# Residual stream by tokens instead of by features in a three-layer transformer kernel on one core

## The chip, the cores and the metric

The kernel runs on one core of a Trainium2 chip. A core has TensorE (PE, matrix products), VectorE (DVE), ScalarE (ACT), GpSimd (POOL) and SyncE (SP, which here issues transfers), each with an instruction stream of its own that it works off in order. The metric is the device time of one execution in microseconds; for the kernel before it is the median of three runs.

## The reference, cut to what matters

512 tokens of 1024 features go through three layers, all in float32. Layer A is attention with a forget gate and a squared-ReLU MLP; layers B and C each have a mixer of two branches and a SwiGLU block. What matters here is what stands at the end of each branch: a product with an output matrix, its addition to the residual stream `x`, and the next normalization over the 1024 features of each token.

```python
# layer A
x = x + g_m * y                                   # y = attention @ fox_w_out
h = rms_norm(x, norm_mlp[i]) * (1 + sc_f) + sh_f
x = x + g_f * (jnp.square(jax.nn.relu(h @ w_mlp_in[i])) @ w_mlp_out[i])
...
# layers B and C
x = x + gate_m * rmsnorm(mixers[layer](h), post_m)
h = rmsnorm(x, pre_f) * (1.0 + scale_f) + shift_f
x = x + gate_f * rmsnorm(swiglu(h, *ffns[layer]), post_f)
```

`rms_norm` divides by the root of the mean square over a token's features. In B and C the branch's output `y` is normalized too, before it is added.

## The kernel before

**Products.** Every float32 matrix is held as two float32r parts, `hi` and `lo`, and a product is three matmuls, hi by hi (L116), hi by lo (L117), lo by hi (L118). A weight unit is loaded by SyncE (`wraw`), rounded by ScalarE (`whi`, L148) and its rest formed by VectorE (`wlo`, L149); names with an x are a second ring. "Feature-major" means features on the partitions and tokens along the row (`fm`, L165), "token-major" the reverse (`tm`, L173).

**The residual stream** `x` and the branch's sum `yacc` are feature-major, 8 chunks of 128 features by 512 tokens. The normalized `h` is kept feature-major as pairs `h_hi`, `h_lo`, since the next products contract over features.

**The six places.** Twice per layer, in its middle (mixer to MLP or SwiGLU) and at its end (to the next layer's mixer, or to the output), `down_halves` (L1283) makes a branch's last product by halves of 256 tokens: per half eight chunks of 24 matmuls with 256 columns. VectorE takes each chunk out of PSUM (L1334, in A L709), ScalarE squares it, GpSimd adds the squares up (L356), the last square stays apart. `total` (L318) then sums over the partitions on TensorE with matrices of ones, three matmuls (L327, L328, L330) and for the last square two passes. `rstd` makes the reciprocal root from a logarithm, an exponential and one Newton step. In B and C `post` (L1265) adds the normalized `yacc` to `x` and sums squares again; `modulate` (L359) forms `u` (L373), `h_hi` (L374, ScalarE) and `h_lo` (L378). While the second half goes through these steps, TensorE has the next block's products with the first half's tokens: `two_blocks` (L1307) computes seven output chunks by halves (`by_halves`) and one in full width.

**What sets the order.** A list scheduler writes each engine's stream by the order in which the program emits instructions and by priority. `behind(n)` lets what is emitted in it give way to the next n instructions; the table `LAG` holds n for the totals, by place and half. Scratch tiles (`t`) come from one ring of `nt` buffers of 512 columns. PSUM has four banks `mm`, in the MLP and SwiGLU phases three `mm2` and one `tot`.

## Time and profile before

| | us |
|---|---|
| median of three runs | 2395.36 |
| lowest and highest | 2389.12, 2403.04 |
| the profiled execution, span from first to last instruction | 2392.9 |
| TensorE busy | 2262.0 |
| VectorE busy | 1508.8 |
| ScalarE busy | 1062.9 |
| GpSimd busy | 439.5 |

TensorE's mean granted clock over the span is 0.970 of full speed. The page gives no separate time of the profiled execution, so its span stands for it; it lies inside the spread of the three runs. A busy share is an average over stages: what matters at the six places is which engine the others wait for there, and whether TensorE, which works in order, stands still.

### The profile page before, as it was taken

To read this page: it belongs to the slowest core of one execution; us is meant where nothing else is said; L and a number is where in the kernel's file an instruction comes from. 1 tells how busy PE (TensorE), PEld (TensorE's weight loads), DVE (VectorE), ACT (ScalarE), POOL (GpSimd) and SP (SyncE) were. 2 spreads that over 40 slices of the span, in tenths; PEclk is the share of its full clock that TensorE was granted. 3 is DMA by queue.
4 is the path that set the end of the run, shared out by engine and by line. 5 is a ranking of instruction groups with operands and counts; after the bars stand their busy time and mean duration, and the time that the engine had idled before them with its cause. 6 is when DMAs were issued, how large, how long until landed. Compare 5 with 4: busy or idle time off the path is not lost.

```text
span 2392.9 us, 35221 instructions
## 1 busy us (share of the span) xinstructions
PE 2262.0 (95%) x13328; PEld 1963.2 (82%) x13328; DVE 1508.8 (63%) x3180; ACT 1062.9 (44%) x2089; POOL 439.5 (18%) x446
## 2 busy tenths in 40 slices
PE   5999998999999898999999999799999998999997
PEld 5898888788898676888888889767888888888887
DVE  6888876664536997675654655735888457422424
ACT  4677654344334554254432233344666344332222
POOL 3333230100013310322000001412343012000002
PEclk7999999999999999999999999899999999999999
DMA  7344326655533223033364652342011242331411
GB/s 249 113 145 138 98 84 199 223 195 166 176 108 88 69 65 56 1 118 94 115 220 150 200 178 80 87 121 79 30 45 33 92 137 71 106 106 60 134 55 61
DMA packets 246090, 271.88 MB, mean 114 GB/s; under 512 B 18736, under 2 KB 204752, under 8 KB 245920
## 3 DMA queue, kind: packets, MB, share of 16 engines
q1 hardware_dynamic: 238192, 254.03, 33.6%
q0 software_dynamic: 3424, 11.26, 2.0%
q10 hardware_dynamic: 4304, 4.34, 0.6%
q8 instruction: 105, 1.72, 0.3%
q14 instruction: 65, 0.53, 0.1%
HBM read 261.16 MB, written 8.42 MB: 113 GB/s over the span
## 4 chain that ended last, share of the span: by engine, by line
PE 75%; DVE 14%; ACT 4%; DMA 3%; issue 2%; POOL 1%; SPq 0%; POOLq 0%; DVEq 0%; ACTq 0%
PE mm L116 21%; PE mm L118 21%; PE mm L117 21%; PE tp L431 2%; DVE wlo L149 1%; DMA wraw<-l_w_in 1%; DVE u L1275 1%; DVE p L421 1%; PE mm L1734 1%; ACT whi L148 1%; PE mm L1657 1%; PE o L470 1%; DVE u L373 1%; PE o L469 1%; PE mm L605 1%
## 5 line engine op out<-in xcount | busy, mean ns | idle before, releaser
L116 PE MATMUL mm<-h_hi,whi 128*128 128x512 f32 (+2 forms) x1056 | 373.8, 356 | 17.9 <-ACT h_hi L374 12.6
L117 PE MATMUL mm<-h_lo,whi 128*128 128x512 f32 (+2 forms) x1056 | 373.3, 354 | 0.2 <-DVE h_lo L378 0.2
L118 PE MATMUL mm<-h_hi,wlo 128*128 128x512 f32 (+2 forms) x1056 | 372.9, 353 | 0.1
L148 ACT CAST whi<-wraw 128x1024 fp32r<-128x1024 f32 (+1 forms) x196 | 199.7, 1023 | 228.4 <-PE mm L117 146.7
L149 DVE TENSOR_TENSOR wlo<-wraw,whi 128x1024 fp32r<-128x1024 f32 (+3 forms) x172 | 210.0, 1224 | 137.2 <-ACT whi L148 136.0
L116 PEld LDWEIGHTS mm<-h_hi,whi 128*128 128x128 f32 (+1 forms) x1056 | 202.5, 193 | 49.9 <-ACT h_hi L374 14.4
L118 PEld LDWEIGHTS mm<-h_hi,wlo 128*128 128x128 f32 (+1 forms) x1056 | 203.8, 193 | 28.1 <-DVE wlo L149 0.5
L116 PE MATMUL mm<-h_hi,whix 128*128 128x512 f32 (+1 forms) x648 | 224.8, 348 | 1.4 <-DVE yacc L1334 1.4
L117 PEld LDWEIGHTS mm<-h_lo,whi 128*128 128x128 f32 (+1 forms) x1056 | 204.0, 193 | 26.6 <-DVE h_lo L378 0.5
L117 PE MATMUL mm<-h_lo,whix 128*128 128x512 f32 (+1 forms) x648 | 224.1, 346 | 0.0
L118 PE MATMUL mm<-h_hi,wlox 128*128 128x512 f32 (+1 forms) x648 | 223.8, 346 | 0.0
L116 PE MATMUL mm<-whi,h_hi 128*128 128x256 f32 x672 | 202.7, 302 | 0.3 <-DVE mod_modA L823 0.3
L117 PE MATMUL mm<-wlo,h_hi 128*128 128x256 f32 x672 | 194.8, 290 | 0.2 <-DVE wlo L149 0.2
L118 PE MATMUL mm<-whi,h_lo 128*128 128x256 f32 x672 | 194.2, 290 | 0.3 <-DVE h_lo L799 0.2
L117 PE MATMUL mm<-hid,whi 128*128 128x512 f32 (+1 forms) x544 | 185.8, 342 | 3.8 <-DVE hid L112 3.8
L116 PE MATMUL mm<-hid,whi 128*128 128x512 f32 (+1 forms) x544 | 187.0, 347 | 1.0 <-ACT hid L109 1.0
L149 DVE TENSOR_TENSOR wlox<-wraw,whix 128x1024 fp32r<-128x1024 f32 x106 | 135.0, 1281 | 81.0 <-ACT whix L148 79.5
L118 PE MATMUL mm<-hid,wlo 128*128 128x512 f32 (+1 forms) x544 | 185.5, 342 | 0.0
L148 ACT CAST whix<-wraw 128x1024 fp32r<-128x1024 f32 x106 | 109.0, 1034 | 143.4 <-PE mm L117 96.9
L246 DVE SCALAR_TENSOR_TENSOR ada_acc<-ada,cols,ada_acc 128x512 f32<-128x512 f32 x182 | 136.3, 749 | 50.9 <-DMA ada<-l_ada_w 43.5
L116 PE MATMUL mm<-hid,whix 128*128 128x256 f32 (+1 forms) x432 | 145.5, 337 | 2.1 <-DVE x L709 2.1
L117 PE MATMUL mm<-hid,whix 128*128 128x256 f32 (+1 forms) x432 | 145.0, 336 | 0.0
(466 smaller groups left out, 5248.9 us busy)
## 6 DMA issues: line engine op xcount, KB each, us to landing
ada<-l_ada_w SPq DMA_DIRECT2D x192, 256.0 KB, 4.5
wraw<-l_w_in SPq DMA_DIRECT2D x54, 512.0 KB, 3.8
wraw<-l_w_gate SPq DMA_DIRECT2D x44, 512.0 KB, 4.2
wraw<-l_w_up SPq DMA_DIRECT2D x44, 512.0 KB, 4.1
wraw<-l_w_down SPq DMA_DIRECT2D x40, 512.0 KB, 3.5
wraw<-w_mlp_in SPq DMA_DIRECT2D x32, 512.0 KB, 4.0
wraw<-w_mlp_out SPq DMA_DIRECT2D x32, 512.0 KB, 3.6
hid<-w_ada SPq DMA_DIRECT2D x48, 256.0 KB, 5.5
```

The costliest lines, as they stand in the source:

```text
L116: mm(ps, a[0], b[0], start=start, stop=False)
L117: mm(ps, a[0], b[1], start=False, stop=False)
L118: mm(ps, a[1], b[0], start=False, stop=stop)
L148: nc.scalar.copy(hi[:, :nk, :n], raw[:, :nk, :n])
L149: e.tensor_sub(lo[:, :nk, :n], raw[:, :nk, :n], hi[:, :nk, :n].bitcast(F32))
L246: nc.vector.scalar_tensor_tensor(acc, raw, c, acc, op0=OP.mult, op1=OP.add)
L373: nc.vector.scalar_tensor_tensor(u, x[:, k, t], gs[:, k:k + 1], r, op0=OP.mult, op1=OP.mult)
L421: nc.vector.tensor_scalar(p[:, :n], p[:, :n], st[:, 2:3], None, op0=OP.mult)
L431: nc.tensor.transpose(tp[:w, j * 128:(j + 1) * 128], p[:, j * 128:j * 128 + w], self.ident)
L469: nc.tensor.matmul(o[:, oc], a, pt[:, j, 0, c], start=first and j == 0, stop=False)
L470: nc.tensor.matmul(o[0:64, oc], a[:, 0:64], pt[:, j, 1, c], start=False, stop=False)
L605: nc.tensor.matmul(S[:, :n], qs[hi, e, tb], kl[hi, :n], start=False, stop=False)
```

## The change

`x` and `yacc` become token-major: 4 blocks of 128 tokens, each a row of 1024 features per token. `down_blocks` replaces `down_halves`: by pairs of token blocks, for each half of the features and each block a token-major product of 24 matmuls with 512 columns. A block's evictions add to `yacc` or `x`; ScalarE squares 512 features and accumulates them per token into a column of `stats`; `token_rsqrt` makes the reciprocal root of that column on VectorE in eleven operations. Gate and gain vectors, which were columns, are needed as rows on all partitions: `row` writes them to DRAM, `on_all` loads them broadcast, both on GpSimd's queue. `normalized` scales a block of `x` by its column on ScalarE into two tiles `xn`, and `modulate` transposes the tiles of a pair of blocks on TensorE into `tot`, from where ScalarE (`h_hi`) and VectorE (`u`, `h_lo`) make the feature-major pairs.

The other products that add to `yacc` (`down`, `out_early`) turn token-major too, with 512 columns as before. Weight units of more than 256 columns hold 2 rows of 128 by 512 columns instead of 4 by 256. `two_blocks` makes six chunks by halves and two in full width; the PSUM banks are two `mm2` and two `tot`. The ring of scratch tiles is 8 in layer A's MLP (12 before) and 8 in the SwiGLU phases (7 before). The host lays out `x` in both ways and reads the output token-major.

```diff
-LAG = ((50, 150), (100, 150), (120, 160), (60, 290), (60, 100), (60, 190))
+LAG = ((110, 130), (110, 130), (110, 130), (110, 130))
+AT, NT = 8, 8
...
+        step = 2 if sum(c1 - c0 for c0, c1 in cols) > 256 else 4
+        for i, k0 in enumerate(range(ks[0], ks[1], step)):
+            out += self.unit(w, k0, min(step, ks[1] - k0), cols, aux[i] if isinstance(aux, tuple) else aux, gain)
...
+    def squares(self, st, i, v):
+        junk = self.t("sq")
+        self.nc.scalar.activation(junk, v, AF.Square, accum_out=st[:, i:i + 1])
+    def token_rsqrt(self, st):
+        nc = self.nc
+        v, h, r, t = [st[:, i:i + 1] for i in (2, 3, 4, 5)]
+        nc.vector.tensor_add(v, st[:, 0:1], st[:, 1:2])
+        nc.vector.tensor_scalar(h, v, -0.5 / D, -0.5 * EPS, op0=OP.mult, op1=OP.add)
+        ri = r.bitcast(I32)
+        nc.vector.tensor_scalar(v, h, -2.0, None, op0=OP.mult)
+        nc.vector.tensor_scalar(ri, v.bitcast(I32), 1, None, op0=OP.arith_shift_right)
+        nc.vector.tensor_scalar(ri, ri, -1.0, float(0x5F3759DF), op0=OP.mult, op1=OP.add)
+        for _ in range(3):
+            nc.vector.tensor_scalar(t, r, r, h, op0=OP.mult, op1=OP.mult)
+            nc.vector.scalar_tensor_tensor(r, t, 1.5, r, op0=OP.add, op1=OP.mult)
+        return r
+    def stats(self):
+        return self.tmp.tile([128, 6], F32, name="stats", bufs=6)
+    def modulate(self, xns, gs, sh, pair, lag=0):
+        nc = self.nc
+        t = slice(pair * 256, pair * 256 + 256)
         us = []
         for k in range(KD + MLAG):
             if k < KD:
+                if k % 2 == 0:
+                    ps = self.tot.tile([128, 2, 256], F32, name="tot")
+                    with self.behind(lag):
+                        for e in range(2):
+                            c = (k + e) % 4 * 128
+                            for b in range(2):
+                                nc.tensor.transpose(ps[:, e, b * 128:b * 128 + 128], xns[b][k // 4][:, c:c + 128], self.ident)
+                p = ps[:, k % 2]
                 u = self.t("u")[:, :256]
                 us.append(u)
+                nc.scalar.activation(self.h[k][0][:, t], p, AF.Identity, scale=gs[:, k:k + 1], bias=sh[:, k:k + 1])
+                nc.vector.tensor_scalar(u, p, gs[:, k:k + 1], sh[:, k:k + 1], op0=OP.mult, op1=OP.add)
             if k >= MLAG:
+                hi, lo = self.h[k - MLAG]
+                nc.vector.tensor_sub(lo[:, t], us[k - MLAG], hi[:, t].bitcast(F32))
+    def normalized(self, x, b, st):
+        r = self.token_rsqrt(st)
+        out = []
+        for c in range(2):
+            out.append(self.t("xn"))
+            self.nc.scalar.activation(out[-1], x[:, b, c * 512:c * 512 + 512], AF.Copy, scale=r)
+        return out
+    def row(self, name, cols):
+        d = self.dram.tile([KD, 128], F32, name=f"row_{name}")
+        self.nc.gpsimd.dma_start(d.rearrange("k p -> p k"), cols)
+        return d
+    def on_all(self, d):
+        t = self.tmp.tile([128, D], F32, name="row", bufs=1)
+        self.nc.gpsimd.dma_start(t, d.rearrange("(o k) p -> o (k p)", o=1).to_broadcast([128, D]))
+        return t
...
+    def gated(self, x, row, early=None):
+        nc = self.nc
+        def evict(b, c, ps, st):
+            f = slice(c * 512, c * 512 + 512)
+            u = self.t("u")
+            if early and c:
+                nc.vector.tensor_add(u, early[b], ps)
+                ps = u
+            nc.vector.tensor_mul(u, ps, row[:, f])
+            nc.vector.tensor_add(x[:, b, f], x[:, b, f], u)
+            self.squares(st, c, x[:, b, f])
         return evict
...
+        ready, late = self.two_blocks([load(0), load(1)], h)
+        y = self.aux.tile([128, 4, D], F32, name="yacc")
...
+                row = self.on_all(self.row("gA5", self.mod("modA", 5)))
+                self.down_blocks(w2, g * 8, hid, self.gated_sum(x, y, row), after)
...
-        self.ph = self.phase("mlpA", (("mm2", 3), ("tot", 1)), nt=12)
-        x = self.reload(a["x"])
+        self.ph = self.phase("mlpA", (("mm2", 2), ("tot", 2)), nt=AT)
+        x, rowA = self.reload(a["xt"]), self.on_all(rowA)
...
+        def mid(b, st):
+            self.xn[b % 2] = self.normalized(x, b, st)
+            if b % 2:
+                self.modulate(self.xn, gs2, self.mod("modA", 3), b // 2, LAG[0][b // 2])
+        self.down_blocks(a["fox_w_out"][0], 0, cat, self.gated(x, rowA, self.early), mid, done=FE)
...
+        def go(b, st):
+            if b == 0:
                 self.mv = self.mod_vectors(l)
-            self.modulate(x, self.mv["gm"], self.mv["sm"], half, ss, lag and lag[half])
-            self.spill(x, d, half)
+            self.xn[b % 2] = self.normalized(x, b, st)
+            self.spill(x, d, b)
+            if b % 2:
+                self.modulate(self.xn, self.mv["gm"], self.mv["sm"], b // 2, lag[b // 2])
...
+    def post(self, x, y, row, b, st, sums=True):
+        nc = self.nc
+        r = self.token_rsqrt(st)
+        st = self.stats() if sums else None
+        for c in range(2):
+            f = slice(c * 512, c * 512 + 512)
+            u = self.t("u")
+            nc.vector.scalar_tensor_tensor(u, y[:, b, f], r, row[:, f], op0=OP.mult, op1=OP.mult)
+            nc.vector.tensor_add(x[:, b, f], x[:, b, f], u)
+            if sums:
+                self.squares(st, c, x[:, b, f])
+        return st
...
+    def down_blocks(self, w, k0, xs, evict, after, gain=None, done=0):
+        first = [0, done]
+        ws = [self.weights(w, (k0 + first[c], k0 + KD), [(c * 512, c * 512 + 512)], c == 1, gain) for c in range(2)]
+        self.xn = [None, None]
+        for pair in range(2):
+            st = [self.stats() for _ in range(2)]
+            for c in range(2):
+                for e in range(2):
+                    b = pair * 2 + e
+                    ps = self.mm.tile([128, T], F32, name="mm")
+                    self.tm(ps, ws[c], 0, 512, xs[first[c]:], b)
+                    evict(b, c, ps, st[e])
+                    if c:
+                        after(b, st[e])
...
+        ps = [[self.mm.tile([128, T], F32, name="mm") for _ in range(4)], [self.mm2.tile([128, T], F32, name="mm2") for _ in range(2)]]
+        part = lambda pp, w, cs: [(p, w[i // 2], i % 2 * 128) for p, i in zip(pp, cs)]
+        self.by_halves([part(ps[0], ws[0], range(4)), part(ps[1], ws[1], (0, 2))], xs)
+        def late(i):
+            p = self.mm.tile([128, T], F32, name="mm")
+            self.fm(p, ws[1][i // 2], i % 2 * 128, i % 2 * 128 + 128, xs)
+            return p
+        return [ps[0], [ps[1][0], None, ps[1][1], None]], late
...
-        self.ph = self.phase(f"ffn{l}", (("mm2", 3), ("tot", 1)), nt=7)
-        x = self.reload(d)
-        def mid(half, ss):
-            ss = self.post(x, y, m["pm"], half, ss, LAG[2][half])
-            self.modulate(x, m["gf"], m["sf"], half, ss, LAG[3][half])
-        self.down_halves(w, 0, cat, self.add_to(y), "ssy", mid, self.col["ssm_g" if l == 0 else "gla_g"])
+        self.ph = self.phase(f"ffn{l}", (("mm2", 2), ("tot", 2)), nt=NT)
+        x, pm = self.reload(d), self.on_all(pm)
...
+        def mid(b, st):
+            st = self.post(x, y, pm, b, st)
+            self.xn[b % 2] = self.normalized(x, b, st)
+            if b % 2:
+                self.modulate(self.xn, m["gf"], m["sf"], b // 2, LAG[2][b // 2])
+        self.down_blocks(w, 0, cat, self.add_to(y), mid, self.col["ssm_g" if l == 0 else "gla_g"])
+        pf = self.on_all(self.row(f"pf{l}", m["pf"]))
         self.next_modulation(l + 1)
         self.ada_lag = ADA
-        go = self.into(x, l + 1, LAG[5])
+        go = self.into(x, l + 1, LAG[3])
         self.ffn(self.h, *[a[f"l{l}_{n}_2"] for n in ("w_gate", "w_up", "w_down")], y,
-                 lambda half, ss: go(half, self.post(x, y, m["pf"], half, ss, LAG[4][half], self.has(l + 1))))
+                 lambda b, st: go(b, self.post(x, y, pf, b, st, self.has(l + 1))))
```

The order of instructions at the second half of B's middle shows the move. TensorE before, among the next block's products with the first half's tokens; `tot_11664` is the total of the second half's squares of `yacc`:

```order
L118 MATMUL mm_11816<-h_hi_61,wlo_11777 128x256
L116 MATMUL mm_11817<-h_hi_61,whi_11776 128x256
L327 MATMUL tot_11664<-ss_hi_11660,onesr_86 128x256 [waits Activation_49]
L117 MATMUL mm_11817<-h_lo_62,whi_11776 128x256
L118 MATMUL mm_11817<-h_hi_61,wlo_11777 128x256
L328 MATMUL tot_11664<-ss_lo_11661,onesr_86 128x256 [waits DVE_49]
L116 MATMUL mm_11818<-h_hi_61,whi_11788 128x256
L330 MATMUL tot_11664<-sq_last_11657,onesr_86 128x256
L117 MATMUL mm_11818<-h_lo_62,whi_11788 128x256
L118 MATMUL mm_11818<-h_hi_61,wlo_11789 128x256
```

TensorE after, at the same point; `xn_11172` and `xn_11237` are the normalized blocks 2 and 3, `mm_11346` and the next are the SwiGLU's first chunks for these tokens:

```order
L119 MATMUL mm2_11351<-h_hi_61,wlox_11343 128x256
L399 MATMUL tot_11241<-ident_82,xn_11237 128x128 [waits Activation_49]
L399 MATMUL tot_11241<-ident_82,xn_11172 128x128
L399 MATMUL tot_11241<-ident_82,xn_11237 128x128
L399 MATMUL tot_11252<-ident_82,xn_11237 128x128
L399 MATMUL tot_11252<-ident_82,xn_11172 128x128
L399 MATMUL tot_11252<-ident_82,xn_11237 128x128
L117 MATMUL mm_11346<-h_hi_61,whi_11300 128x256 [waits Activation_49]
L117 MATMUL mm_11347<-h_hi_61,whi_11300 128x256
```

The total of three matmuls, which stood between products that need nothing of it, is gone. The transposes (two more for block 2 stand seventeen rows ahead) stand behind all products with the first pair's tokens, and the products behind them need their result. What the rows wait for stands in brackets.

VectorE before, at the end of the update of `x` in the second half, with the root of the total `tot_11725`:

```order
L1275 SCALAR_TENSOR_TENSOR u_11711<-yacc_9672,pm0_7391,r_11659 128x256
L1278 TENSOR_TENSOR x_10991<-x_10991,u_11711 128x256
L112 TENSOR_TENSOR ss_lo_11722<-ssx_11674,ss_hi_11721 128x256
L306 SCALAR_TENSOR_TENSOR nr_11731<-r_11720 128x256
L307 SCALAR_TENSOR_TENSOR nr_11731<-tot_11725,nr_11731 128x256
L308 SCALAR_TENSOR_TENSOR r_11720<-nr_11731,r_11720 128x256
L373 SCALAR_TENSOR_TENSOR u_11735<-x_10991,gf0_7389,r_11720 128x256
L373 SCALAR_TENSOR_TENSOR u_11738<-x_10991,gf0_7389,r_11720 128x256
```

VectorE after, for block 3: `stats_11054` is the column of the branch's output, `stats_11215` that of `x` after the update:

```order
L1339 SCALAR_TENSOR_TENSOR u_11216<-yacc_9425,stats_11054,row_10747 128x512
L1340 TENSOR_TENSOR x_10744<-x_10744,u_11216 128x512
L1339 SCALAR_TENSOR_TENSOR u_11221<-yacc_9425,stats_11054,row_10747 128x512
L1340 TENSOR_TENSOR x_10744<-x_10744,u_11221 128x512
L372 TENSOR_TENSOR stats_11215<-stats_11215 128x1
L373 TENSOR_SCALAR stats_11215<-stats_11215 128x1
...
L379 TENSOR_SCALAR stats_11215<-stats_11215 128x1
L380 SCALAR_TENSOR_TENSOR stats_11215<-stats_11215 128x1
L404 TENSOR_SCALAR u_11246<-tot_11241,gf0_7141,mod_mod0_4827 128x256
L407 TENSOR_TENSOR h_lo_62<-u_11246,h_hi_61 128x256
```

Each column `stats` is worked on by eleven rows, of which the excerpt leaves out seven in the second one. In the stream before, three operations of 256 columns stood in its place.

## Rows read from the trace of the kernel before

**Rows 1.** The page, busy time of each engine in the whole span.

```profile
span 2392.9 us, 35221 instructions
...
PE 2262.0 (95%) x13328; PEld 1963.2 (82%) x13328; DVE 1508.8 (63%) x3180; ACT 1062.9 (44%) x2089; POOL 439.5 (18%) x446
```

**Rows 2.** The page, shares of the chain that ended last.

```profile
PE 75%; DVE 14%; ACT 4%; DMA 3%; issue 2%; POOL 1%; SPq 0%; POOLq 0%; DVEq 0%; ACTq 0%
```

**Rows 3.** TensorE's waits over the whole span: us in total, times, longest.

```profile
PE tot L327 <- ACT ss_hi L109: 21.7, 8, 4.5
PE mm L116 <- ACT h_hi L374: 12.6, 4, 3.5
...
PE mm L116 <- DVE x L709: 3.0, 2, 2.1
...
PE mm L116 <- DVE yacc L1334: 1.8, 2, 1.4
```

**Rows 4.** Timeline of TensorE, 512 columns: start us, modelled us; 35 rows between.

```profile
1439.64 0.39 PE L117 MATMUL mm<-h_lo,whi 128*128 128x512 f32 x1
...
1447.80 0.39 PE L117 MATMUL mm<-h_lo,whi 128*128 128x512 f32 x1
```

**Rows 5.** Timeline of TensorE, 256 columns, 42 rows between.

```profile
1475.76 0.28 PE L117 MATMUL mm<-hid,whix 128*128 128x256 f32 x1
...
1480.92 0.28 PE L118 MATMUL mm<-hid,wlox 128*128 128x256 f32 x1
```

**Rows 6.** Timeline of TensorE, a total over partitions and the product after it.

```profile
1482.65 0.28 PE L327 MATMUL tot<-ss_hi,onesr 128*128 128x256 f32 x1
...
1483.13 0.47 PE L116 MATMUL mm<-hid,whi 128*128 128x256 f32 x1
```

**Rows 7.** Timeline of TensorE, two groups of four 128x128 transposes.

```profile
984.39 0.60 PE L1235 MATMUL mm<-ident,y 128*128 128x128 f32 x4
984.83 0.60 PE L1166 MATMUL mm<-ident,hid 128*128 128x128 f32 x4
```

**Rows 8.** Timeline of mixer B: squares on ScalarE, column chain on VectorE.

```profile
1038.84 0.63 ACT L1226 ACTIVATE z<-y 128x512 f32<-128x512 f32 x1 [1.96 <-DVE y L1224]
...
1039.38 0.18 ACT L1226 ACTIVATION_READ_ACCUMULATOR z<-y 128x1 f32 x1
...
1039.60 0.15 DVE L1227 TENSOR_SCALAR st<-st 128x1 f32<-128x1 f32 x1 [0.19 <-ACT z L1226]
...
1041.48 0.58 DVE L882 SCALAR_TENSOR_TENSOR st<-rs_t,rs_y 128x1 f32<-128x1 f32 x1
```

**Rows 9.** Costliest groups of VectorE by shape: xcount | busy us, mean ns.

```profile
L149 DVE TENSOR_TENSOR wlo<-wraw,whi 128x1024 fp32r<-128x1024 f32 x164 | 206.1, 1260 | 134.6 <-ACT whi L148 133.4
...
L1334 DVE TENSOR_TENSOR yacc<-yacc,mm 128x256 f32<-128x256 f32 x64 | 26.3, 415 | 51.4 <-PE mm L118 51.4
...
L709 DVE SCALAR_TENSOR_TENSOR x<-mm,mod_modA,x 128x512 f32<-128x512 f32 x24 | 17.9, 748 | 15.6 <-PE mm L118 15.5
...
L1368 DVE TENSOR_TENSOR yacc<-yacc,mm 128x512 f32<-128x512 f32 x16 | 10.9, 682 | 10.8 <-PE mm L118 10.8
```

**Rows 10.** Timeline of TensorE, a wait at B's middle.

```profile
1132.90 0.58 PE L327 MATMUL tot<-ss_hi,onesr 128*128 128x256 f32 x1 [3.56 <-ACT ss_hi L109]
```

**Rows 11.** Busy time by stretch: length, PE (x) ..., PEclk, DMA.

```profile
1132.00:1136.00 4.00, 3.10 (x12) 2.92 (x13) 0.42 (x1) 1.08 (x3) 0.41 (x1) 0.50 0.43 127
1456.00:1568.00 112.00, 98.31 (x726) 93.25 (x725) 72.08 (x140) 43.17 (x88) 36.46 (x49) 0.94 0.32 91
1940.00:2060.00 120.00, 109.67 (x814) 105.38 (x813) 79.32 (x159) 58.20 (x119) 22.83 (x26) 0.97 0.36 110
```

**Rows 12.** Timeline of the tail: last product, last addition.

```profile
2378.68 0.28 PE L118 MATMUL mm<-hid,wlox 128*128 128x256 f32 x1
...
2389.16 0.42 DVE L1278 TENSOR_TENSOR x<-x,u 128x256 f32<-128x256 f32 x1
```

**Rows 13.** DMA issues: queue, xcount, KB each, median us to landing.

```profile
x<-sp_l POOLq DMA_DIRECT2D x4, 1024.0 KB, 8.0
```

More of the change, by code (lines that the diff above doesn't have):

```diff
@@ L143, in unit @@
             return out
-        hi, lo = self.ring(aux)
+        hi, lo = (wide(t) for t in self.ring(aux))
         if gain is None:
@@ L279 @@
     mv = None
+    row_p = None
     ada_tile = None
@@ L516, in fox_early @@
         self.finish()
[L517 to L525 removed]
+        wk = self.weights(w, (0, FE), [(512, 1024)])
+        for b in range(4):
+            ps = self.mm.tile([128, T], F32, name="mm")
+            self.tm(ps, wk, 0, 512, cat[:FE], b)
+            out.append(self.hid.tile([128, T], F32, name="hid"))
+            self.nc.scalar.copy(out[-1], ps)
+            yield
     def fox_gates(self, h):
@@ L1283, in down_halves @@
-    def down_halves(self, w, k0, xs, evict, name, after, gain=None, done=0):
-        first = [0, 0, done, done]
-        ws = [self.weights(w, (k0 + first[q], k0 + KD), [(q * 256, q * 256 + 256)], q >= 2, gain) for q in range(4)]
-        for half in range(2):
-            t0, t1 = half * 256, half * 256 + 256
-            ss = self.sums(name)
-            for m in range(KD):
-                ps = self.mm.tile([128, T], F32, name="mm")
-                self.fm(ps, ws[m // 2], m % 2 * 128, m % 2 * 128 + 128, xs[first[m // 2]:], t0, t1)
-                v = evict(m, ps[:, t0:t1], slice(t0, t1))
-                sums = self.add_squares(ss, v, m)
-            after(half, sums)
+        r = self.token_rsqrt(st)
@@ new lines, in post, with down @@
+        st = self.stats() if sums else None
+        for c in range(2):
+            f = slice(c * 512, c * 512 + 512)
+            u = self.t("u")
+            nc.vector.scalar_tensor_tensor(u, y[:, b, f], r, row[:, f], op0=OP.mult, op1=OP.mult)
+            nc.vector.tensor_add(x[:, b, f], x[:, b, f], u)
+            if sums:
+                self.squares(st, c, x[:, b, f])
+        return st
+    def down(self, w, k0, xs, y, first, step):
+        for c in range(2):
+            wk = self.weights(w, (k0, k0 + len(xs)), [(c * 512, c * 512 + 512)], aux=c == 1)
+            for b in range(4):
+                ps = self.mm.tile([128, T], F32, name="mm")
+                self.tm(ps, wk, 0, 512, xs, b)
+                v = y[:, b, c * 512:c * 512 + 512]
+                if first:
+                    self.nc.scalar.copy(v, ps)
+                else:
+                    self.nc.vector.tensor_add(v, v, ps)
+                self.step(step)
@@ L1348, in ffn @@
                     self.step()
-                    gate, up = [ready[p][i] if p < 2 else self.chunk(ws, i, h) for i in (c, 2 + c)]
+                    gate, up = [(ready[p][i] or late(i)) if p < 2 else self.chunk(ws, i, h) for i in (c, 2 + c)]
                     s = self.t("f", F32)
```

163 lines of the change are left out of this document (45 added, 118 removed).

## Prediction

> **What bounds the kernel now.** I read the page's busy times first. TensorE is busy for 2262.0 of 2392.9 us, VectorE for 63%, GpSimd for 18% [rows 1]; the reader is to see that work taken from GpSimd or ScalarE can't show in the time unless something waits for it. The chain of waits says the same from the other side: three quarters of it is TensorE, 14% is VectorE [rows 2]. So a change pays in two coins only: the time that TensorE needs to issue its matmuls, and the time that it stands still. The list of TensorE's waits gives the second. The largest are those of the totals L327 for `ss_hi` (21.7 us in 8) and of the next products for the first `h_hi` of a half (12.6 us in 4), with 3.0 for `x` and 1.8 for `yacc` from evictions: 39.1 us, all at the six places where a residual branch ends and the next block begins [rows 3]. The table by stretches places them: at B's end TensorE is idle for 13.7 of 112 us, at C's middle for 10.3 of 120 [rows 11]. These are the places that the change rewrites.
>
> **TensorE's own time.** The order counts 2352 matmuls of 256 columns fewer in the products at the six places (2208 in the last products, 144 in the blocks by halves that become full-width) and 1176 of 512 more. A matmul's modelled duration is longer than its slot, so I take start to start: 36 steps of 512 columns take 8.16 us, 0.2267 each [rows 4]; 43 steps of 256 take 5.16, 0.120 each [rows 5]. 2352 x 0.120 = 282.2 becomes 1176 x 0.2267 = 266.6: -15.6 us. The 18 totals go, each 0.48 from its first matmul to the product behind it [rows 6]: -8.6. The 160 transposes come, 0.44 for four [rows 7]: +17.6. Sum -6.6.
>
> Against the largest of these terms, the Trainium skill (TensorE: Matmul & The Clock Gate, Back-to-back issue gap) gives an isolated gap of N/2.4 + 2.5 ns; an estimate from it is 216 ns at 512 columns and 109 at 256. By that, two narrow matmuls would cost only 3 ns more than a wide one, the term would be 1176 x 0.003 = -3.5 instead of -15.6, and the sum would end 12 us later. The rows differ from it in both widths and decide, since they are these products on this chip.
>
> **VectorE at the six places.** Per token the sum of squares now comes from ScalarE's accumulator: 0.63 for 512 columns and 0.18 for reading it, and the reciprocal root from eleven VectorE operations on one column. The trace has nine steps of such a chain between 1039.60 and 1041.48, 0.21 each [rows 8]; eleven are 2.3, with the hand-over 2.4 us. There are 36 chains (4 blocks x 9), 86 us of VectorE. The long operations keep their price: 0.68 to add 512 columns, 0.75 for scale-and-add, 0.42 for 256 columns, 1.26 for a weight split [rows 9]. GpSimd loses its 108 additions of squares; it was 18% busy, so I count nothing for them. ScalarE loses the narrow squares, 36 logarithms and exponentials, also nothing. The gate and gain rows now come by six broadcasts on GpSimd's queue, behind the reload of `x`, and are first needed by the first block's update. No row shows such a broadcast; the nearest is the reload itself, 8.0 us for 1 MB [rows 13]. It is between 0 and 8 us late at each of the three middles; with the first update 16 us (three products of 5.4) after the queue opens I take 0.
>
> What TensorE waits for is now a normalized block. Take the second pair of token blocks at B's middle. Behind the first pair's last `h_lo`, VectorE's order has for blocks 2 and 3 two chains each, two multiplications and two additions each: 4 x 2.4 + 4 x 0.75 + 4 x 0.68 = 15.3. In two spots a chain must first get ScalarE's squares of the addition just before it, 2 x 0.8, and after the last chain ScalarE normalizes the first half of the block, 0.63 as for the square: 17.5 us in one row. TensorE has the first pair's half of six products as cover, 6 x 24 x 0.120 = 17.3, but it begins them while VectorE still makes `h_lo`: 8 times one 256-column operation from PSUM and one subtraction, 8 x 0.83 = 6.6. So 10.7 us cover 17.5 and TensorE stands 6.8 us. C's middle is the same; B's end has two token-major values products and four chunks, the same 17.3, so 6.8 too. In A there is one chain per block: the last block needs about three 0.68 operations, 0.8, 2.4 and 0.6, 5.9 us, which fits under the cover; with the splits and evictions that stand in the same row I put 3 at its middle and 2 at its end. 25 us for the second pairs.
>
> The first pairs have the whole of products 5 to 8 as cover (4 x 24 x 0.2267 = 21.8 us), but their transposes stand inside the last of them. There VectorE has the chains of blocks 0 and 1 (4 x 2.4 with their eight long operations 15.3) and, in the same row, three evictions (2.0) and about three splits of the next weights (3.8): 21, plus the waits for ScalarE. I take 5 us each at B's and C's middle, 2 at B's end and at A's middle, 1 at A's end: 15. So 40 us of new waits stand against the 39.1 that go: +1. The bounds of this term are -39 (all is covered) and +25 (below, the slower case); I take 40, since it has each duration from a row and each queue from the order.
>
> A long wait also costs clock: after the wait of 3.6 us at B's middle [rows 10] the next 4 us ran at a granted clock of 0.50, the 1.2 GHz level, and took 12 matmuls in 3.10 busy us where 12 x 0.120 = 1.4 would do [rows 11], 1.7 us. Before and after have about as many such waits; I count nothing.
>
> **The tail.** Before, from the last product's last matmul (2378.68) to the last addition's end (2389.58) are 10.9 us, and 3.3 more to the span's end for the store [rows 12], 14.2 in all. After, block 2's chain stands ahead of block 3's eviction. Block 2's last product ends one product (5.4) earlier; from 4.8 us before the last matmul: eviction 0.68, squares 0.9, chain 2.4, two multiplications 1.5, two additions 1.4 end at +2.1. Then block 3: 0.68, 0.9, 2.4, 1.5, 1.4 end at +8.9, and the same 3.3 make 12.2: -2.0.
>
> **The sum.** -6.6 - 2.0 + 1 = -7.6, so the profiled span would go from 2392.9 to 2385.3. The span is 2.5 us below the median of the runs, 2395.4; for a median I say 2388.
>
> **Rivals.** Half a per cent, 12 us, is about what a measurement of this kernel tells from no change.
> 1. The chains hide. For it: they wait on nothing but themselves, and the scheduler may find them gaps; VectorE is idle for over a third of the span [rows 1]. Against it: the order puts them in one row behind one another. If a chain weighs on the others by a third of its length (0.8 instead of 2.4), the four at B's middle give back 6.4, nearly the whole 6.8, the same at B's end and C's middle (19 us), and the first pairs there another 9: 28 us less, 2360. The Trainium skill (Vector Engine (DVE) Microarchitecture Reference, 5.2) states about 75 ns of fixed cost per instruction after queue overlap, measured on back-to-back instructions; an estimate for eleven is 0.84. The trace's dependent column operations start 0.21 apart instead, which is why this is not the forecast. All waits gone would be 2348.
> 2. VectorE binds the transitions: slower. The place is the row ahead of blocks 2 and 3. If the four splits of the next weights (4 x 1.26 = 5.0) land ahead of these chains at B's middle, B's end and C's middle, rather than behind them, TensorE waits 15 us more, and each of five long waits is followed by a stretch at half clock, 1.7 each, 8.5: +23.5, 2412. It decides from the point at which the chain of pair 1 starts over 5 us after the first pair's last `h_lo`. For it: VectorE's rows leave no gap there by the sum above; against it: in the order these splits stand behind the chains.
> 3. Late weights: slower or even. A first product now needs all eight weight rows of 512 columns, four splits, where two units of four rows did before. Two more splits (2.5) at six places are +15: 2403. For it: each split sits on the engine that is now crowded; against it: the weights can be fetched during the group before.
>
> **Chances.** The forecast 0.46, with its own range of 2376 to 2402: 0.12 of that is faster by over 0.5%, 0.29 within it, 0.05 slower. Rival 1 has 0.28, all faster. Rival 2 has 0.18: 0.16 slower, 0.02 within. Rival 3 has 0.08: 0.06 slower, 0.02 within. Together: faster 0.40, same 0.33, slower 0.27. The range goes from 2352, near the end of rival 1, to 2415, beyond rival 2.
>
> **What would show it.** The list of TensorE's waits has neither `ss_hi` nor a wait of a total, and instead transposes waiting for `xn` from ScalarE, the longest at B's middle, B's end and C's middle, about 7 us each. Wide matmuls keep 0.227, transposes 0.11. A column chain measures 2.3 to 2.5. The last matmul lies 12 us ahead of the end. Wrong would be: waits for `xn` below 2 us each (rival 1), above 10 (rival 2), or first products waiting for `wlo` (rival 3).

## The result, and the profile after

The changed kernel takes 2412.6 us (median of six runs, 2409.6 to 2414.4) where the kernel before takes 2397.4 (also of six): 1.0059 times as long, 95% interval 1.0042 to 1.0077. The forecast was 2388 and the time lies inside the range (2352 to 2415), but on the wrong side: 0.6% slower instead of 0.3% faster. The profiled execution took 2410.4, its span is 2408.4, 15.5 us more than before.

The busy times, to be held against [rows 1]:

```profile
PE 2257.3 (94%) x12240; PEld 1903.6 (79%) x12240; DVE 1534.7 (64%) x3383; ACT 1062.4 (44%) x2043; POOL 340.3 (14%) x339
```

TensorE's matmuls are fewer by 1088, as counted (2352 - 1176 + 72 of the 18 totals - 160), and GpSimd lost over a fifth of its work. TensorE's waits, against [rows 3] (total, times, longest):

```profile
PE tot L399 <- ACT xn L415: 42.7, 12, 10.2
...
PE mm L117 <- ACT hid L110: 8.8, 2, 8.5
...
PE tot L399 <- DVE u L404: 4.3, 2, 4.1
...
PE tot L275 <- POOL hid L269: 2.5, 2, 2.2
```

The waits for `ss_hi` are gone and transposes wait for `xn` instead, 42.7 us against a forecast of 40. The three rows below that are the news: a wait of 8.5 us for a hidden chunk of layer A's MLP, which is not at any of the six places, one of 4.1 at A's end, and one of 2.2 for the modulation's sums, also in layer A's MLP. Added up over the whole list, TensorE's waits are 138.0 us where they were 116.8.

The timeline of the 8.5 us, engine by engine (GpSimd, VectorE, ScalarE, TensorE), in the first group of layer A's MLP:

```profile
425.58 1.17 POOL L421 DMA_DIRECT2D row_gA<-mod_modA  x1 [2.42 <-DVE mod_modA L279]
437.53 0.55 POOL L427 DMA_DIRECT2D row<-row_gA  x1 [10.78 <-DMA row_gA<-mod_modA]
```

```profile
438.68 0.75 DVE L249 SCALAR_TENSOR_TENSOR ada_acc<-ada,cols,ada_acc 128x512 f32<-128x512 f32 x1 [7.89 <-DMA ada<-l_ada_w]
```

```profile
440.62 0.62 ACT L268 COPY fs<-ada_acc 64x512 f32<-64x512 f32 x1 [15.06 <-DVE ada_acc L249]
441.14 0.59 ACT L794 ACTIVATE f<-mm 128x512 f32<-128x512 f32 x1
```

```profile
443.09 0.80 PE L117 MATMUL mm<-whi,hid 128*128 128x512 f32 x1 [8.52 <-ACT hid L110]
```

It reads from top to bottom. GpSimd writes the gain row gA5 to DRAM: 4 KB, but turned from columns into a row, 1024 elements of 4 bytes. The load behind it waits 10.8 us for it, and in the same time the next layer's modulation weights (`ada`, on SyncE's queue) don't come: VectorE stands 7.9 us. ScalarE's next instruction is the copy of that sum, so it stands 15.1 us, and only then makes the hidden chunk for which TensorE stands. In the stretch 432 to 440 the DMA engines are shown busy over half the time, while they move 47 and 67 GB/s:

```profile
432.00:436.00 4.00, 2.56 (x12) 1.78 (x10) 0.00 (x0) 0.00 (x0) 0.00 (x0) 1.00 0.74 47
436.00:440.00 4.00, 0.00 (x0) 0.00 (x0) 0.92 (x2) 0.00 (x0) 0.55 (x1) 0.65 0.55 67
```

(Columns as in [rows 11]: PE, PEld, DVE, ACT, POOL, clock, DMA share, GB/s.)

### The profile page after: what moved, and what is told of

It is laid out like the page before. It is cut to its first block, busy times and chain, and to the rows that moved or that the text cites. A ratio compares the mean times of both kernels' runs of the same rounds, so it can differ in the third digit from the quotient of the medians.

```text
span 2408.4 us, 32973 instructions
## 1 busy us (share of the span) xinstructions
PE 2257.3 (94%) x12240; PEld 1903.6 (79%) x12240; DVE 1534.7 (64%) x3383; ACT 1062.4 (44%) x2043; POOL 340.3 (14%) x339
## 5 line engine op out<-in xcount | busy, mean ns | idle before, releaser
L117 PE MATMUL mm<-h_hi,whi 128*128 128x512 f32 (+4 forms) x928 | 333.2, 364 | 5.2 <-DVE yacc L1415 2.0
L118 PE MATMUL mm<-h_lo,whi 128*128 128x512 f32 (+4 forms) x928 | 333.6, 360 | 0.6 <-DVE h_lo L407 0.5
L119 PE MATMUL mm<-h_hi,wlo 128*128 128x512 f32 (+4 forms) x928 | 332.7, 359 | 0.0
L151 DVE TENSOR_TENSOR wlo<-wraw,whi 128x1024 fp32r<-128x1024 f32 (+1 forms) x169 | 210.5, 1250 | 120.3 <-ACT whi L150 119.6
L117 PE MATMUL mm<-whi,h_hi 128*128 128x256 f32 (+1 forms) x736 | 227.4, 310 | 0.3 <-DVE mod_modA L888 0.3
L118 PE MATMUL mm<-wlo,h_hi 128*128 128x256 f32 (+1 forms) x736 | 219.6, 299 | 0.2 <-DVE wlo L151 0.2
L119 PE MATMUL mm<-whi,h_lo 128*128 128x256 f32 (+1 forms) x736 | 218.9, 298 | 0.3 <-DVE h_lo L864 0.2
L118 PEld LDWEIGHTS mm<-h_lo,whi 128*128 128x128 f32 (+3 forms) x928 | 176.0, 190 | 27.4 <-DVE h_lo L407 1.5
L119 PEld LDWEIGHTS mm<-h_hi,wlo 128*128 128x128 f32 (+3 forms) x928 | 175.9, 190 | 27.4 <-issue 0.4
L117 PE MATMUL mm<-whi,hid 128*128 128x512 f32 x416 | 166.9, 401 | 8.8 <-ACT hid L110 8.8
L119 PE MATMUL mm<-whi,hid 128*128 128x512 f32 x416 | 163.7, 397 | 2.6 <-DVE hid L113 2.5
```

The lines of the kernel that those rows point to most:

```text
L117: mm(ps, a[0], b[0], start=start, stop=False)
L118: mm(ps, a[0], b[1], start=False, stop=False)
L119: mm(ps, a[1], b[0], start=False, stop=stop)
L151: e.tensor_sub(lo[:, :nk, :n], raw[:, :nk, :n], hi[:, :nk, :n].bitcast(F32))
```

## The experiments

The kernel before has medians between 2393.4 and 2397.4 us in the four sets of runs, so the gains below are differences of ratios to it, times its 2396 us; the changed kernel stands at 1.0059. By the intervals of the two ratios such a gain is uncertain by 5 to 8 us. The theories: **W**, the element-wise writes of the six rows hold back other transfers; **the ring**, the scratch ring of 8 buffers in layer A's MLP (12 before) delays its hidden chunks; and the forecast's own mechanism, the chains of column operations, of unknown share.

**1. Rows written contiguously.** `a_rows_block`: the order of instructions on every engine stays, only the form of six writes and of their loads changes. The features stand permuted in these rows, so the results are other numbers.

```diff
-        d = self.dram.tile([KD, 128], F32, name=f"row_{name}")
-        self.nc.gpsimd.dma_start(d.rearrange("k p -> p k"), cols)
+        d = self.dram.tile([128, KD], F32, name=f"row_{name}")
+        self.nc.gpsimd.dma_start(d, cols)
```

> The changed kernel with the six gate and gain rows written to DRAM in the order of the partitions (32 bytes per partition) instead of by single 4-byte elements; the rows so come in a permuted order of the features, nothing else differs. Theory W (the element-wise write of layer A's row, which took 11.7 us to land, held up the loads of the modulation, and through VectorE and ScalarE TensorE, 8.5 us, with half clock behind it): that wait of a hidden chunk falls below 2 us and the time by 8 to 12 us, to 2400 to 2405. Theory R (the ring of 8 scratch tiles instead of 12 lets too few modulation loads run ahead): the wait stays above 6 us and the time within 3 us of 2412.

Measured: 2393.9, ratio 0.9986 (0.9966 to 1.0007): 17.5 us less than the changed kernel, more than the 8 to 12 expected of the one wait. The wait of 8.5 for the hidden chunk is gone, and that for `u` is down to 0.6; what stays:

```profile
PE tot L399 <- ACT xn L415: 39.3, 12, 10.2
...
PE mm L119 <- DVE hid L113: 2.8, 2, 2.5
```

The way the rows are written costs more than the whole loss of the change. That the other numbers in the rows make the difference is not excluded by this run alone; experiment 11, which computes the same as the changed kernel, bears on it.

**2. The ring.** `b_ring8`: the kernel before with 8 scratch buffers in layer A's MLP.

```diff
-        self.ph = self.phase("mlpA", (("mm2", 3), ("tot", 1)), nt=12)
+        self.ph = self.phase("mlpA", (("mm2", 3), ("tot", 1)), nt=8)
```

> The kernel before with 8 instead of 12 scratch tiles in layer A's MLP, nothing else. Theory R: waits for modulation loads in the first group of the MLP grow and the time is 6 to 12 us above the kernel before, 2403 to 2409. Theory W: within 3 us of the kernel before.

Measured: 2394.3, ratio 1.0004 (0.9986 to 1.0023). The ring falls, the more so as experiment 1 lost the wait with its ring still at 8.

**3. One write more in the kernel before.** `b_row`: the element-wise write of gA5, whose result nobody reads.

```diff
+                d = self.dram.tile([KD, 128], F32, name="row_gA5")
+                nc.gpsimd.dma_start(d.rearrange("k p -> p k"), gate)
```

> The kernel before, and in layer A the gate vector is also written to DRAM by single 4-byte elements, at the point where the changed kernel writes it; nobody reads it. Theory W: the write lands after about 10 us, the modulation loads behind it are late, and the time grows by 4 to 10 us. Theory R: within 2 us of the kernel before.

Measured: 2394.7, ratio 0.9998 (0.9976 to 1.0020): no cost, and the expected 4 to 10 us missed. The write did there what it does in the changed kernel (DMA, the stretch 418 to 440; then VectorE):

```profile
ada<-l_ada_w SPq DMA_DIRECT2D x11, 256.0 KB, 6.7
...
row_gA<-mod_modA POOLq DMA_DIRECT2D x1, 4.0 KB, 10.3
```

```profile
428.99 0.75 DVE L246 SCALAR_TENSOR_TENSOR ada_acc<-ada,cols,ada_acc 128x512 f32<-128x512 f32 x1 [3.49 <-DMA ada<-l_ada_w]
```

The modulation's weights are late again and VectorE waits for them, but from 418 to 460 us TensorE has no wait of 1 us or more. Here, too, a hidden chunk stands behind ScalarE's copy of this sum, but the copy is not late: the sum is ready at 429.7, while ScalarE is held until 430.1 by the rounding of a weight unit that stands ahead of the copy and waits for a matmul (in the kernel before without the write it waits 9.9 us in the same way):

```profile
430.08 1.04 ACT L148 CAST whi<-wraw 128x1024 fp32r<-128x1024 f32 x1 [11.38 <-PE mm L117]
431.15 0.62 ACT L265 COPY fs<-ada_acc 64x512 f32<-64x512 f32 x1
```

The write's price is thus not its own duration but what stands, two queues further, behind what it delays.

**4. Chains without their root.** `a_root_free`: the changed kernel with two column operations in place of eleven; the reciprocal root is left out.

```diff
         nc.vector.tensor_add(v, st[:, 0:1], st[:, 1:2])
-        nc.vector.tensor_scalar(h, v, -0.5 / D, -0.5 * EPS, op0=OP.mult, op1=OP.add)
...
-            nc.vector.scalar_tensor_tensor(r, t, 1.5, r, op0=OP.add, op1=OP.mult)
+        nc.vector.tensor_scalar(r, v, 1e-9, 0.03, op0=OP.mult, op1=OP.add)
```

> The changed kernel with the root left out: two column operations (sum, and a constant plus almost nothing of it) instead of eleven, all else and the order of dependences kept. Theory C (the waits of the transposes for the normalized blocks, 42.7 us, are made of VectorE's column chains): these waits fall to below 12 us and the time by 28 to 40 us, to 2372 to 2384. Rival: the waits are made of ScalarE's squares, VectorE's long operations and weight splits, and fall by less than 15 us; the time stays above 2395.

Measured: 2349.2, ratio 0.9803 (0.9773 to 0.9832), 61 us less than the changed kernel, 47 less than the kernel before, and well beyond the 28 to 40 expected. In the list of waits 1.3 us for `xn` stay of 42.7, and 6.9 for the hidden chunk, since the writes are as they were:

```profile
PE mm L117 <- ACT hid L110: 6.9, 1, 6.9
...
PE tot L392 <- ACT xn L408: 1.3, 1, 1.3
```

So the chains do lie on the path. TensorE's waits fall by 44 us (138.0 to 93.6), the tail by 3 (from 11.4 to 8.3), and with the waits goes time at the low clock, 11 us (53.4 to 42.3, counted as under "The half clock" below); these make some 58 of the 60 us by which the spans differ. That the time is near the forecast's case without waits (2348) is luck: the element-wise writes still cost here, and the wait for `u` at A's end is 6.7 us instead of 4.1.

**5. A row turned on TensorE.** `v_rows`, computing the same: gA5 and the two pf rows are transposed on TensorE, copied by ScalarE and written in pieces of 512 bytes.

```diff
+            nc.tensor.transpose(ps[:KD, :128], cols, self.ident)
+            s = self.t("rs")[:KD, :128]
+            nc.scalar.copy(s, ps[:KD, :128])
+            nc.gpsimd.dma_start(d, s)
...
+            if g == 2:
+                rowd = self.row_t("gA5", self.mod("modA", 5))
```

> The changed kernel; layer A's gate row and the two rows of the SwiGLU's gain are transposed on TensorE and written to DRAM as eight pieces of 512 bytes, at a later point of the program, instead of by 4-byte elements. Theory W (the element-wise writes cost what separates the changed kernel from the one before): 0.995 to 1.002 of the kernel before, and no wait of a hidden chunk above 3 us in layer A. Rival (the permuted rows gained by other data or by luck of the order): within 5 us of the changed kernel, 1.004 and more of the one before.

Measured: 2410.8, ratio 1.0064 (1.0042 to 1.0085): nothing gained, the rival's time and not W's. The wait at 443 is gone, that for `u` at A's end is down from 4.1 us to 0.9 and the first one for `xn` at B's end from 5.8 to 2.3, but a new one stands at 573, again with the modulation's copy ahead of the chunk on ScalarE:

```profile
572.14 0.62 ACT L268 COPY fs<-ada_acc 64x512 f32<-64x512 f32 x1 [3.92 <-DVE ada_acc L249]
```

```profile
573.30 0.79 PE L117 MATMUL mm<-h_hi,whi 128*128 128x512 f32 x1 [5.43 <-ACT f L806]
```

GpSimd's queue shows the row of the next mixer's post gain, still element-wise, issued 22 us earlier than in the changed kernel (568.4 against 590.9) together with the new row, and landing after 11.7 us, with the modulation's weights behind it at 7.3. That fits W with another write in the role; the two writes were not tried apart. The list also has 44.3 us for `xn`, 5.0 more than in experiment 1; they arise at B's and C's middle (the longest there 10.2 instead of 8.4), and their cause was not tried. TensorE's waits so add up to 135.0, hardly less than the 138.0 of the changed kernel. What the run leaves open is whether permuted rows gain by themselves.

**6. One chain for two blocks.** `a_merge`, computing the same: the two blocks of a pair share one chain of 14 operations on two columns instead of two chains of 11 (not at the output, where block 2 would wait for block 3).

```diff
-        v, h, r, t = [st[:, i:i + 1] for i in (2, 3, 4, 5)]
-        nc.vector.tensor_add(v, st[:, 0:1], st[:, 1:2])
+        v, h, r, t = [st[:, i, es] for i in (2, 3, 4, 5)]
+        nc.vector.tensor_add(v, st[:, 0, es], st[:, 1, es])
...
-                    if c:
-                        after(b, st[e])
+                    if c and pair not in merge:
+                        after(pair, st, slice(e, e + 1))
+            if pair in merge:
+                after(pair, st, slice(0, 2))
```

> The changed kernel; the roots of the two token blocks of a pair are taken in one chain of 14 operations on two columns instead of two chains of 11 on one, except at the output. Per pair and norm VectorE has 2.7 instead of 4.8 us. Theory C (chains make the waits of the transposes): the waits for normalized blocks fall from 43 us to 25 to 33 and the time by 8 to 16 us against the changed kernel, to about 1.000 of the kernel before. Rival (what counts is when the last block's chain can start): block 2's work is put off until block 3 is there, the waits stay at 40 or more, and the time stays at 1.005 and more.

Measured: 2393.0, ratio 0.9988 (0.9976 to 0.9999), 17 us less than the changed kernel (8 to 16 were expected). The waits for `xn` fall from 42.7 to

```profile
PE tot L400 <- ACT xn L416: 24.9, 8, 9.4
```

A merged chain takes 2.74 us for its two columns, from the first row's start to the last one's end, where two chains take 2 x 2.43:

```profile
1148.11 0.16 DVE L370 TENSOR_TENSOR stats<-stats 128x2 f32<-128x2 f32 x1 [0.85 <-ACT sq L366]
...
1150.69 0.16 DVE L383 SCALAR_TENSOR_TENSOR stats<-stats 128x2 f32<-128x2 f32 x1
```

**7 and 8. Both.** `v_merge` has the rows of experiment 5 and the chains of 6; `v_merge1` merges only the second pair's.

```diff
-MERGE = (0, 1)
+MERGE = (1,)
```

> Both edits, the transposed rows and the merged chains. If their effects add: 0.992 to 0.996 of the kernel before.

> The transposed rows, and the merged chains for the second pair of blocks alone. The first pair has a product's time between its blocks, which a merged chain gives away; theory C with that: 1 to 4 us faster than with both pairs merged, 0.990 to 0.995 of the kernel before.

Measured: 2388.7, ratio 0.9958 (0.9944 to 0.9972), and 2391.3, ratio 0.9983 (0.9966 to 1.0001). The first lies in its range. The second misses: it was to be 1 to 4 us faster than with both pairs merged and is 6 slower, just clear of the intervals, so what a merged chain gives away at the first pair is less than what it saves. The moved wait stays in both (9.9 and 7.7 us for `f`).

**9 and 10. Which rows.** `a_gA5_block` and `a_pf_block`: experiment 1 for gA5 alone, and for the two pf rows alone.

```diff
+        if name[:2] in ('gA',) and name != "gA2":
+            d = self.dram.tile([128, KD], F32, name=f"row_{name}")
+            self.nc.gpsimd.dma_start(d, cols)
```

> The changed kernel with only the gain row gA5 of layer A written as 32 contiguous bytes per partition (its features then stand permuted in that row); the other five rows are written element by element as in the changed kernel. With all six rows written so the time fell from 2412.6 to 2393.9. Theory 'one write in layer A': the write of gA5 holds back the loads of the modulation behind it, ScalarE's copy waits for the modulation, and the two late hidden chunks wait behind that copy. Then the waits of TensorE for hid at 419 to 443 us (13.2 us in the changed kernel) shrink to under 4, and the time falls by 10 to 14 us, to 2398 to 2403. Rival 'the rows at the branch ends': what costs is that pm and pf come late or hold the weights at the ends of the branches; then this kernel gains 3 us or less, 2410, and the waits for hid stay.

> The changed kernel with only the rows pf (of mixers B and C) written as 32 contiguous bytes per partition (features permuted in these rows). Theory 'one write in layer A': only the weight unit at B's end, whose cast waits 4.6 us in the changed kernel, comes earlier; the longest wait of TensorE for xn, 10.2 us at 1555.7, falls to about 5, and the time falls by 3 to 7 us, to 2406 to 2409. Rival 'the rows at the branch ends': 10 us or more, under 2402, with shorter waits at all three places where a pf row is written or loaded.

Measured: ratio 1.0016 (0.9997 to 1.0035), 10 us gained by gA5; 1.0024 (1.0011 to 1.0038), 8 us gained by pf. Together 18.7, against 17.5 for all six rows: the first theory's size for gA5 was right; that for pf (3 to 7) looks too small, but 8 us lies between it and the rival's 10, and the runs can't tell them apart. In the stretch 425 to 438, the changed kernel first, then `a_gA5_block` (issues, KB, us to landing):

```profile
ada<-l_ada_w SPq DMA_DIRECT2D x5, 256.0 KB, 10.2
...
row_gA<-mod_modA POOLq DMA_DIRECT2D x1, 4.0 KB, 11.7
```

```profile
ada<-l_ada_w SPq DMA_DIRECT2D x11, 256.0 KB, 3.2
...
row_gA<-mod_modA POOLq DMA_DIRECT2D x1, 4.0 KB, 2.5
```

The same 4 KB in runs of 32 bytes land in 2.5 us instead of 11.7, and the modulation's weights beside them in 3.2 instead of 10.2, with eleven issued where five were. The single packets in the trace show the same: while the element-wise write is under way (428.5 to 437.3) SyncE's packets of 2 KB take 0.39 us on average and up to 4.2, in `a_gA5_block` (425 to 438) 0.095 and up to 0.6. The Trainium skill (DMA: Bandwidth & Descriptors, Rules for kernel authors) says that a non-contiguous last dimension becomes one descriptor per element. The two landings are in line with it, though no record here counts descriptors: the write is sixteen packets of 256 bytes in either form. The Trainium skill (DMA: Bandwidth & Descriptors, Queues, rings and completion order) has each DMA engine take turns between its queues, a whole packet at a time. How a turn is divided no run here shows; the rows show that SyncE's loads take three times as long.

What pf costs is at A's and B's end. Only the latter had been expected. ScalarE in the changed kernel, and the waits of TensorE that follow:

```profile
742.13 1.05 ACT L150 CAST whi<-wraw 128x1024 fp32r<-128x1024 f32 x1 [6.90 <-DMA wraw<-l_w_in]
...
746.48 1.09 PE L399 MATMUL tot<-ident,xn 128*128 128x128 f32 x4 [4.05 <-DVE u L404]
```

```profile
1518.44 1.04 ACT L150 CAST whi<-wraw 128x1024 fp32r<-128x1024 f32 x1 [4.60 <-DMA wraw<-l_w_in]
...
1524.42 1.54 PE L399 MATMUL tot<-ident,xn 128*128 128x128 f32 x6 [5.78 <-ACT xn L415]
```

Both weight units were late behind the writes at 727.4 and 1503.5. In `a_pf_block` the first waits 3.6 and the second not at all:

```profile
737.20 1.05 ACT L150 CAST whi<-wraw 128x1024 fp32r<-128x1024 f32 x1 [3.56 <-DMA wraw<-l_w_in]
...
741.61 0.63 PE L399 MATMUL tot<-ident,xn 128*128 128x128 f32 x4 [0.77 <-DVE u L404]
```

```profile
1505.42 1.04 ACT L150 CAST whi<-wraw 128x1024 fp32r<-128x1024 f32 x1
...
1512.56 0.88 PE L399 MATMUL tot<-ident,xn 128*128 128x128 f32 x6 [2.25 <-ACT xn L415]
```

The gain at B's end was looked for in the wrong wait, too: the 10.2 us of the second pair stay, the first pair's wait there goes from 5.8 to 2.3 (1524.42 and 1512.56).

**11 and 12. The writes at another time.** `a_late`, computing the same: gA5 and the pf rows pass through one VectorE operation that also reads (times zero) a tile finished later, so that their writes leave in the middle of the MLP and of the mixers. `m_late` has the merged chains of 6 in addition.

```diff
+    def row_after(self, name, cols, tile):
+        c = self.const.tile([128, KD], F32, name=f"late_{name}")
+        self.nc.vector.scalar_tensor_tensor(c, tile[:, :KD].bitcast(F32), 0.0, cols, op0=OP.mult, op1=OP.add)
+        return self.row(name, c)
...
+            if g == 1:
+                rowd = self.row_after("gA5", self.mod("modA", 5), hid[0][0])
...
+        pfd = self.row_after(f"pf{l}", m["pf"], cat[0][0])
```

> The changed kernel, computing the same, with the same six element-wise writes, but two kinds of them later: gA5 is first copied on VectorE in an operation that also reads (times zero) a hidden chunk of the MLP's second group, and the pf rows in one that reads a chunk of the mixer's output in the same way, so that the writes leave for DRAM in the middle of the MLP and of the mixer. Theory 'a write costs by what stands behind it': the loads of the modulation and the weights at B's end are no longer behind a write, TensorE's waits for hid at 419 to 443 go, and the time is that of the contiguous rows within 5 us, 2392 to 2399. Rival 'an element write costs wherever it is': weight loads in the MLP or in the mixer are late instead, VectorE's or ScalarE's waits for wraw grow there, and the time stays above 2406.

> The kernel a_late with, in addition, one chain of column operations on two columns for each pair of token blocks (the last branch's output excepted), computing the same. If the cost of the rows and that of the chains are separate waits, the gains add up: -19.5 for the chains (2412.6 to 2393.0 as measured) and about -16 for the rows, 2377, 0.8% below the kernel before. Rival: the two overlap (the chain's wait hides behind late rows or weights), then about 2389, as with the rows transposed on TensorE and merged chains.

Measured: 2399.1, ratio 1.0013 (1.0000 to 1.0026), 11 us gained where 14 to 20 were expected; the time is at the upper edge of what was expected. Three writes leave at another time, and the numbers are the same, so this gain is not one of other numbers. The waits at 443 and at A's end go, but the new place of gA5's write (476.5) again has modulation weights behind it: VectorE waits 8.0 us for them, and TensorE loses 3.2 at

```profile
493.78 0.79 PE L117 MATMUL mm<-h_hi,whix 128*128 128x512 f32 x1 [3.20 <-ACT f L798]
```

With merged chains: 2373.6, ratio 0.9901 (0.9882 to 0.9919). That beats both kernels, the one before by 1%, and by more than the two gains added (17 + 11 us from 1.0059 would be 0.9942). The 10 us beyond the sum are just clear of the intervals. Expected of separate gains were 2377, from 19.5 and 16 us. Why they more than add was not tried; the list shows the waits for `xn` at 16.3, below the 24.9 of `a_merge`:

```profile
PE tot L400 <- ACT xn L416: 16.3, 8, 7.3
```

## Why the prediction was wrong

**The step that failed** is the sentence on the gate and gain rows: "six broadcasts on GpSimd's queue ... between 0 and 8 us late ... I take 0". The broadcasts were indeed not late: VectorE waits for no `row` at any middle. What the sum left out is the other half of the step, the six writes that make these rows in DRAM. They are only 4 KB each and were put at nothing without a reason; they cost 17.5 us (experiment 1), some 10 of them from gA5 and 8 from pf (9 and 10). The rows themselves are in time: the writes delay transfers of another queue, and TensorE waits behind those, in layer A's MLP, which the change does not touch, and at A's and B's end. With 17.5 us taken off, the changed kernel is at 0.9986 of the time before (0.9966 to 1.0007), where the forecast said 0.997. In runs that compute the same, the size is less sure: 11 us when three of the writes are moved (experiment 11), 21 in the kernel with merged chains (6 against 12), none when they are remade on TensorE (5).

**Own time of TensorE: the spacings held, the sum fell short.** The widths keep their spacing: nine steps of 512 columns in 2.04 us, 0.227, and fifteen of 256 in 1.80, 0.120, in the changed kernel:

```profile
1429.74 0.39 PE L119 MATMUL mm<-h_hi,wlo 128*128 128x512 f32 x1
...
1431.78 0.39 PE L119 MATMUL mm<-h_hi,wlo 128*128 128x512 f32 x1
```

```profile
1541.15 0.28 PE L119 MATMUL mm<-h_hi,wlo 128*128 128x256 f32 x1
...
1542.95 0.28 PE L119 MATMUL mm<-h_hi,wlo 128*128 128x256 f32 x1
```

Summed over the timeline, start to start and without the waits, the transposes take 21.0 us (17.6 forecast) and the old totals took 13.4 (8.6): 51 of the 160 transposes, and 16 of the 71 matmuls of totals in the trace, stand where the granted clock is 0.5, the 1.2 GHz level. These two errors nearly cancel. The products of 256 and 512 columns, summed in the same way, take 1816.4 us after and 1828.2 before: -11.8 where the forecast has -15.6. Together that is -4.2 instead of -6.6; why the products saved less than their spacings say was not tried.

**Transitions: the sum held, 42.7 against 40, its parts less.** The longest three, B's middle, B's end and C's middle, were forecast at 6.8 each:

```profile
1165.10 1.54 PE L399 MATMUL tot<-ident,xn 128*128 128x128 f32 x6 [8.39 <-ACT xn L415]
...
1555.67 1.54 PE L399 MATMUL tot<-ident,xn 128*128 128x128 f32 x6 [10.17 <-ACT xn L415]
...
2048.97 1.54 PE L399 MATMUL tot<-ident,xn 128*128 128x128 f32 x6 [8.37 <-ACT xn L415]
```

They are larger because the row of four chains at B's middle takes 20.0 us, from its first operation to the transposes at 1165.1, not 17.5: ahead of the third chain VectorE waits for ScalarE, which has block 2's two normalizations ahead of block 3's last square:

```profile
1145.09 0.15 DVE L372 TENSOR_TENSOR stats<-stats 128x1 f32<-128x1 f32 x1
...
1155.69 0.16 DVE L372 TENSOR_TENSOR stats<-stats 128x1 f32<-128x1 f32 x1 [2.08 <-ACT sq L366]
```

The first pairs were forecast too large in turn (1.5 and 1.3 instead of 5 at B's and C's middle), and of the 5.8 at B's end 3.5 go with the pf write. That the sum comes so near is in part luck. The chain itself measures 2.43 us against 2.4, here the last one of the span:

```profile
2400.07 0.16 DVE L372 TENSOR_TENSOR stats<-stats 128x1 f32<-128x1 f32 x1 [0.85 <-ACT sq L366]
...
2402.34 0.16 DVE L380 SCALAR_TENSOR_TENSOR stats<-stats 128x1 f32<-128x1 f32 x1
```

**Tail: held.** From the last matmul to the end are 11.4 us (2397.03 to 2408.4), where 14.2 were before [rows 12] and 12.2 forecast; the last two additions end at 2405.1:

```profile
2397.03 0.39 PE L119 MATMUL mm<-whix,hid 128*128 128x512 f32 x1
```

```profile
2403.86 1.28 DVE L1340 TENSOR_TENSOR x<-x,u 128x512 f32<-128x512 f32 x2
```

**The half clock: held.** Summed over stretches of 2 us, TensorE's busy time times the share of the clock that was not granted is 53.3 us before and 53.4 after. It is 51 to 60 in all the other runs but `a_root_free`, so it can't tell less than some 5 us.

**The rivals.** Rival 2 named a time of 2412, which is what came, by luck, and a wait above 10 us for `xn`, which is there once; but its mechanism did not occur: of the four splits one stands ahead of the chains at B's middle, and with cheap writes the time is 2393.9. Rival 1 (the chains hide) falls: 42.7 us of waits for `xn` are there, and without the chains' root the time is 61 us less. Rival 3 falls: the list has no new wait for `wlo`; weights did come late at A's and B's end, but behind the pf writes.

**The terms together, and what stays open.** The terms as measured, -4.2 for TensorE's own time, -2.8 for the tail and +21.2 for all waits, make +14.2; the spans differ by 15.5. In the kernel before, the tail's last total and the wait ahead of it, 1.5 us together, stand in two of the terms; counted once, the terms agree with the spans. Open are the 3.8 us that the products did not save, the 5 us more of waits for `xn` in experiment 5, why the gains of experiment 12 more than add, and what the rows pm and gA2 cost, which were not tried by themselves.

## What to carry to other kernels

Price each transfer that a change adds twice: once for who waits for it, and once for what it delays in the other queues, down to the engines that work in order behind that. A transposing write of a few KB belongs where no load is due, or in contiguous runs; moved to where another load is due, it moves the wait with it (experiments 5 and 11). A chain of tiny dependent operations costs its latency per chain and not per column, so share it between blocks before looking for a shorter formula.

## What the runs showed of the hardware

A write of 4 KB as 1024 single elements landed in 8.2 to 12.8 us (six of them in the changed kernel), in runs of 32 bytes in 1.7 to 5.6 (the six of `a_rows_block`; 2.5 for gA5), and while that of gA5 was under way loads of 256 KB on another queue took 10.2 us instead of 3.2. Operations of one column that depend on each other start 0.19 to 0.31 us apart on VectorE; a chain of eleven on one column takes 2.43 us, one of fourteen on two columns 2.74.
